# A two-layer hybrid step on one core: the engines' order from the scheduler's finer timing model, with three kinds of loads kept in program order

## The chip, the cores and the metric

The kernel runs on one core of one Trainium2 chip. The core has four compute engines, each with its own in-order queue of instructions: PE (TensorE, matmul), DVE (VectorE), ACT (ScalarE) and POOL (GpSimd). SP (SyncE) issues most of the loads. PE's weight loads are listed apart, as PEld. The metric is device time in microseconds (us) of one execution; lower is better. The time given is the median of several runs, and one further execution is recorded with a profile.

## What is computed

The reference is one inference step of a two-layer trunk on 640 tokens (512 latent, 128 context) of width 1024. Layer 0 mixes tokens with gated attention (16 query heads, 4 key/value heads of width 64), layer 1 with a gated linear recurrence in both directions (8 heads of width 128). Each layer modulates its input by a linear map of a conditioning vector and ends in a layer norm over the scaled residual.

```python
for i in range(DEPTH):
    sh_p, sc_p, g_p = _adaln(c_ctx, ada_w[i], ada_b[i])
    sh_s, sc_s, g_s = _adaln(c, ada_w[i], ada_b[i])
    hp = xp * (1.0 + sc_p) + sh_p
    hs = xs * (1.0 + sc_s) + sh_s
    if i % N_MIXERS == 0:
        out_p, kp, vp = _attn_context(hp, ...)
        out_s = _attn_latent(hs, cache_k, cache_v, ...)
    else:
        out_p, sp_fw, sp_bw = _rec_mix(hp, zeros, zeros, ...)
        out_s, _, _ = _rec_mix(hs, state_fw, state_bw, ...)
    xp = _layer_norm(DEEPNORM_ALPHA * xp + g_p * out_p, ...)
    xs = _layer_norm(DEEPNORM_ALPHA * xs + g_s * out_s, ...)

# _rec_mix, per head and direction, chunk by chunk
o_i = scores(q_i, k_i, decay) @ v_i + (q_i * exp(b_i)) @ S
S = exp(b_last) * S + (k_i * exp(b_last - b_i)).T @ v_i
```

It returns the tokens after both layers, the new keys and values of the context tokens, and the new recurrent states.

## The kernel before

**Number format.** Each fp32 operand of a large product is split into a high part, a cast, and a low part, the remainder. A product is then three matmuls: high by high, low by high, high by low. The function `split_piece` does this for weights: ACT casts a loaded piece `raw` of 128x1024 into the high part (L215), another engine subtracts to get the low part (L216).

**Loads.** Weights come in pieces of 512 KB in one fixed list, `order`, on SP's queue. `pump` issues the next loads of the list whenever fewer than two pieces are waiting (eight at the start). The list holds x and the modulation weights first (`"x"`, `"ada_w0"`, `"attn_kv"`), then the attention's input weights, the rest of the modulation weights (`"ada_w1"` among them), the attention's output weights, and last the recurrence's (`"rec_w_in"`, `"rec_w_out"`).

**Stages.** The lead-in (to about 150 us) transposes and modulates x, projects keys, values and the first queries (rows xps, adaps, acc, qps) and the gate path (gps). The attention (to 387 us) runs units of one head and 256 queries: scores sc, exponentials p, transposes pt, product with the values pot; the next queries (qmm, qps) and the modulation maps (adaps) run between them. Then the output projection, the layer norm and the transposed input of layer 1 follow (outp, h1t).

The recurrent layer (487.7 to 815.1 us in the profile) goes over 8 heads. `proj_gen` projects a head: 5 weight pieces, first two for value and gate (vgps, L1090 to L1092), then three for q and the two forget gates (rps, L1100 to L1102), 48 rps matmuls for each third. `evac` takes a third out of its bank: a sigmoid s on ACT (L1122), for the gates also a second sigmoid s2 (L1132), and products on DVE. The weight pieces use a ring of two buffers (rhi, rlo; one of the pieces goes to wspare), so a cast into rhi needs the matmuls that read the buffer's last content done.

`gla_gen` is a head's lane, which runs beside the next head's projection. It has 7 levels: at each, lv matmuls on PE (L1230, from the sixth level on L1236) read a copy kc of the keys that ACT makes (L1208) and the scaled queries; DVE scales the keys (kv, L1239), squares the decays (L1243), scales the queries (qv, L1244) for the next level, and merges the scores into near (L1220). After the fifth level comes dg (L1254). Then kp transposes the keys (L1270), ACT copies them to kt (L1272), sp takes kt times v (L1276), op forms the output (L1293 to L1296), on is normed and multiplied by the gate on DVE (L1307), and oT transposes it (L1312).

The last head's lane has no projection beside it. The tail (`tail_gen`) runs there: the splits of the output weights, gateps (L288) and 84 outp matmuls of layer 1 for the heads that are ready. Then the last outp matmuls, the layer norm and the stores follow.

**What sets the order.** The program is traced in the order in which the Python code calls its instructions, and a lane is woven into a projection by due times in us (`Lane`, `D_GLA` to `D_OUT`, `weave`). The framework's scheduler then decides the order of each engine's instructions, within what the data allow, by a timing model. `tc.keep_in_program_order(ins)` ties an instruction to the one traced before it on the same engine, so that the two are not exchanged. Some instructions are tied in this way already (L513, L675, L749, L1328 and others).

Of the kernel before, what the change touches and what calls it, by code (L numbers as in the profile page):

```python
# [18 lines left out]
P = 128  # L19
D = 1024  # L20
KT = D // P
TS = 4
# [109 lines left out]
def hybrid_step(ctx: ExitStack, tc: tile.TileContext, a: dict, o: dict):  # L132
    nc = tc.nc
# [54 lines left out]

    ahead = deque()
    order = deque()  # L190

    def pump():
        while order:
            start = order[0] in FIRST
            if len(ahead) >= (RAW_START if start else RAW_AHEAD):
                break
            src = order.popleft()
            if src[0] == "x":
                c = slice(src[1] * CW, (src[1] + 1) * CW)
                nc.sync.dma_start(xt[:, :TS, c], a["xs"][:, c].rearrange("(t p) d -> p t d", p=P))  # L200
                nc.sync.dma_start(xt[:, TS, c], a["xp"][:, c])
                continue
            raw = (raw0 if start else rawp).tile([P, 1024], F32, tag="raw", name="raw")
            nc.sync.dma_start(raw, piece(src))
            ahead.append((src, raw))

    def piece(src):
        name, c, i = src
        return a[name][c][:, i * 1024:(i + 1) * 1024]

    def split_piece(hi, lo, src, lo_eng=None):
        pump()
        got, raw = ahead.popleft()
        assert got == src, (got, src)
        nc.scalar.copy(hi, raw)  # L215
        (lo_eng or nc.gpsimd).tensor_tensor(lo, raw, hi.bitcast(F32), ALU.subtract)  # L216
        pump()
# [28 lines left out]
    def take(src):  # L246
        pump()
        got, raw = ahead.popleft()
        assert got == src, (got, src)
        return raw  # L250
# [118 lines left out]
    def lpool(name, bufs):  # L369
        return left.enter_context(pool(name, bufs))  # L370
# [8 lines left out]
    xt = gsp.tile([P, TT, D], F32, tag="gs", name="xt")  # L379
# [1010 lines left out]
    xp = lpool("xp", 3)  # L1390
# [102 lines left out]
```

## Time and profile before

| | us |
|---|---|
| median of 3 runs (lowest, highest) | 907.76 (903.08, 910.23) |
| the profiled execution, its own time | 908.88 |
| span of its trace | 907.1 |
| mean granted TensorE clock | 0.982 |
| PE's last instruction to the end of the span | 9.3 |

The span is what the trace covers; the 1.8 us between it and the execution's own time lie around it. The page counts busy time per engine: engines work side by side, so the shares do not add up to 100%. "Idle before" is the time an engine stood ahead of an instruction, with the engine that released it. The granted clock is the share of full speed at which TensorE was allowed to run.

### The profile page before, as it was taken

The numbers are of one execution on the slowest core, as the hardware profiler recorded it, in microseconds if no ns is written. First come the engines' busy times: TensorE is split into PE (matmuls) and PEld (weight loads), VectorE is DVE, ScalarE is ACT, GpSimd is POOL, SyncE is SP. The second block draws the span as 40 slices with busy tenths as digits, with TensorE's granted clock in tenths as the row PEclk, the third lists the DMA queues.
The fourth block names the chain that finished last, engine by engine and source line by source line (L and its number), as shares of the span: only waits on it lengthen the run. The fifth ranks groups of instructions, "written<-read, shape, count | busy, mean of one in ns | idle before, by whom it ended". The sixth has DMA issues, their size and how long they took to land.

```text
span 907.1 us, 19250 instructions
## 1 busy us (share of the span) xinstructions
PE 856.6 (94%) x8116; PEld 745.8 (82%) x8116; DVE 542.8 (60%) x966; ACT 374.1 (41%) x735; POOL 213.9 (24%) x251
## 2 busy tenths in 40 slices
PE   5999899989989989999999999999999999998995
PEld 3679899857867845677889999999999999996774
DVE  3466334654655644567634758585858575859485
ACT  1142346543555644632243444444444444344200
POOL 2014001421323443440000133324141404120110
PEclk9999899998999999999999999999999999998998
DMA  9832120024024036264122322323132332223121
GB/s 316 306 127 82 47 70 25 1 92 142 1 91 142 1 118 220 81 209 151 45 95 69 93 84 78 96 59 108 56 101 82 87 91 87 83 70 136 53 94 69
DMA packets 32678, 89.86 MB, mean 99 GB/s; under 512 B 4400, under 2 KB 11568, under 8 KB 32592
## 3 DMA queue, kind: packets, MB, share of 16 engines
q1 hardware_dynamic: 21984, 71.57, 23.3%
q0 software_dynamic: 3264, 9.51, 3.9%
q10 hardware_dynamic: 7344, 7.55, 2.7%
q8 instruction: 64, 1.05, 0.5%
q14 instruction: 22, 0.18, 0.1%
HBM read 79.44 MB, written 9.18 MB: 98 GB/s over the span
## 4 chain that ended last, share of the span: by engine, by line
PE 80%; DVE 7%; DMA 5%; ACT 3%; POOL 3%; issue 2%; SPq 0%; ACTq 0%; DVEq 0%; POOLq 0%
PE rps L1100 7%; PE rps L1101 6%; PE rps L1102 6%; PE vgps L1090 4%; PE pot L744 4%; PE vgps L1091 4%; PE vgps L1092 4%; DMA raw<-in_ada_w 4%; PE pt L826 4%; PE outp L978 3%; PE outp L979 3%; PE outp L980 3%; PE adaps L258 3%; PE lv L1230 2%; PE sc L717 2%; PE gps L315 2%
## 5 line engine op out<-in xcount | busy, mean ns | idle before, releaser
L1100 PE MATMUL rps<-h1hi,rhi 128*128 128x320 f32 x368 | 117.2, 319 | 0.0
L1101 PE MATMUL rps<-h1lo,rhi 128*128 128x320 f32 x368 | 113.6, 309 | 0.0
L1102 PE MATMUL rps<-h1hi,rlo 128*128 128x320 f32 x368 | 113.5, 309 | 0.0
L819 POOL TENSOR_SCALAR p<-p,rc 128x640 f32<-128x640 f32 x64 | 52.1, 816 | 112.2 <-DVE rc L818 109.3
L1100 PEld LDWEIGHTS rps<-h1hi,rhi 128*128 128x128 f32 x368 | 69.1, 188 | 1.3
L814 ACT ACTIVATE p<-sc,nm 128x640 f32<-128x640 f32 x64 | 51.1, 798 | 44.7 <-DVE nm L811 34.4
L1101 PEld LDWEIGHTS rps<-h1lo,rhi 128*128 128x128 f32 x368 | 69.1, 188 | 0.0
L1102 PEld LDWEIGHTS rps<-h1hi,rlo 128*128 128x128 f32 x368 | 69.1, 188 | 0.0
L811 DVE TENSOR_REDUCE nm<-sc 128x1 f32<-128x640 f32 x64 | 52.4, 820 | 24.2 <-PE sc L718 23.5
L216 DVE TENSOR_TENSOR rlo<-raw,rhi 128x1024 fp32r<-128x1024 f32 x32 | 46.1, 1441 | 34.2 <-ACT rhi L215 34.2
L1258 POOL COPY At<-near 32x160 f32<-32x160 f32 x32 | 14.0, 438 | 198.0 <-DVE near L1220 197.0
L1208 ACT COPY kc<-A 128x640 f32<-128x640 f32 x40 | 32.2, 804 | 59.3 <-DVE A L1239 51.4
L215 ACT CAST rhi<-raw 128x1024 fp32r<-128x1024 f32 x32 | 33.6, 1049 | 52.8 <-PE rps L1101 47.7
L826 PE MATMUL pt<-small,p 128*128 128x128 f32 x320 | 52.6, 285 | 1.5 <-DVE pts L722 0.8
L1090 PE MATMUL vgps<-rhi,h1hi 128*128 128x256 f32 x180 | 51.3, 285 | 1.2 <-ACT h1hi L932 1.2
L1092 PE MATMUL vgps<-rhi,h1lo 128*128 128x256 f32 x180 | 50.4, 280 | 0.4 <-DVE h1lo L933 0.4
L1091 PE MATMUL vgps<-rlo,h1hi 128*128 128x256 f32 x180 | 50.6, 281 | 0.0
L744 PE MATMUL pot<-pts,vv 128*64 128x256 f32 x320 | 50.0, 390 | 0.0
L722 ACT COPY pts<-pt 128x512 f32<-128x512 f32 x64 | 36.1, 587 | 32.1 <-PE pt L826 31.8
L826 PEld LDWEIGHTS pt<-small,p 128*128 128x128 f32 x320 | 37.8, 144 | 13.4 <-issue 7.1
L258 PE MATMUL adaps<-raw,sil 128*32 128x256 f32 x384 | 33.7, 429 | 11.2 <-DMA raw<-in_ada_w 10.6
L717 PE MATMUL sc<-kk,X 128*128 128x320 f32 x128 | 43.8, 350 | 0.4 <-ACT p L814 0.4
(261 smaller groups left out, 2436.9 us busy)
## 6 DMA issues: line engine op xcount, KB each, us to landing
raw<-in_ada_w SPq DMA_DIRECT2D x48, 512.0 KB, 5.0
raw<-in_rec_w_in SPq DMA_DIRECT2D x40, 512.0 KB, 3.5
raw<-in_attn_w_in SPq DMA_DIRECT2D x16, 512.0 KB, 4.0
raw<-in_attn_w_out SPq DMA_DIRECT2D x8, 512.0 KB, 3.6
raw<-in_rec_w_out SPq DMA_DIRECT2D x8, 512.0 KB, 3.3
x1d<-y SPq DMA_DIRECT2D x5, 512.0 KB, 3.1
rx<-x1d POOLq DMA_DIRECT2D x20, 128.0 KB, 3.7
x1a<-rx POOLq DMA_DIRECT2D x20, 128.0 KB, 2.6
```

The costliest lines, as they stand in the source:

```text
L258: nc.tensor.matmul(ps[32 * q:32 * q + 32, :CW], sil[:, 4 * i + q, :], raw[:, q * CW:(q + 1) * CW], start=(i == 0), stop=(i == 1))
L717: nc.tensor.matmul(out, X[:, h, t0:t0 + P], kk[:, c, k0:k1], start=True, stop=False)
L744: nc.tensor.matmul(pot[j * HD:(j + 1) * HD, :CW], vv[:, slot, c * HD:(c + 1) * HD], moving[j], start=first, stop=last)
L811: nc.vector.tensor_reduce(nm[:, 0:1], sc[:, :, :320], AX.XY, ALU.max, negate=True)
L819: nc.gpsimd.tensor_scalar(p, p, rs[:, 0:1], 1.0, ALU.mult, ALU.mult)
L826: nc.tensor.transpose(pt[:, i * 256 + q * P:i * 256 + (q + 1) * P], ps[q][:, (k0 + i) * P:(k0 + i + 1) * P], ident)
L1090: nc.tensor.matmul(out, h1hi[:, k, t], hi, start=(k == 0), stop=False)
L1091: nc.tensor.matmul(out, h1hi[:, k, t], lo, start=False, stop=False)
L1092: nc.tensor.matmul(out, h1lo[:, k, t], hi, start=False, stop=(k == KT - 1))
L1100: nc.tensor.matmul(ps[:, j, :320], hi[:, k, :], h1hi[:, k, t], start=(k == 0), stop=False)
L1101: nc.tensor.matmul(ps[:, j, :320], hi[:, k, :], h1lo[:, k, t], start=False, stop=False)
L1102: nc.tensor.matmul(ps[:, j, :320], lo[:, k, :], h1hi[:, k, t], start=False, stop=(k == KT - 1))
```

## The change

Three edits. In `hybrid_step`, `pin` is a short name for `tc.keep_in_program_order` and `pass_on` a function that does nothing. In `pump`, loads of x and of all pieces whose name does not begin with "rec" go through `pin`. In `kernel`, the scheduler is told to decide with its finer timing model. All line numbers from L191 on are one higher in the changed kernel.

```diff
     ahead = deque()
     order = deque()
+    pin, pass_on = tc.keep_in_program_order, lambda ins: ins
...
-                nc.sync.dma_start(xt[:, :TS, c], a["xs"][:, c].rearrange("(t p) d -> p t d", p=P))
-                nc.sync.dma_start(xt[:, TS, c], a["xp"][:, c])
+                pin(nc.sync.dma_start(xt[:, :TS, c], a["xs"][:, c].rearrange("(t p) d -> p t d", p=P)))
+                pin(nc.sync.dma_start(xt[:, TS, c], a["xp"][:, c]))
                 continue
             raw = (raw0 if start else rawp).tile([P, 1024], F32, tag="raw", name="raw")
-            nc.sync.dma_start(raw, piece(src))
+            (pass_on if src[0][:3] == "rec" else pin)(nc.sync.dma_start(raw, piece(src)))
...
-    with tile.TileContext(nc) as tc:
+    with tile.TileContext(nc, schedule_with_timeline_sim=True) as tc:
         hybrid_step(tc, a, o)
```

No instruction is added or removed. Of the rows that each engine runs, 4011 stand elsewhere on PE, 673 on DVE, 325 on ACT, 37 on POOL and none on SP. Three places follow, with the order before and then the order now.

Place 1 is ACT in one head of the recurrent layer, from the fifth level's kc (copy of the keys) to the sigmoids of the second third. Before:

```order
L1208 COPY kc<-A 128x640
L215 CAST wspare<-raw 128x1024
L215 CAST rhi<-raw 128x1024
L1263 COPY At<-lv 32x5x32 x4
L1122 ACTIVATE s<-rps 128x640
L1263 COPY At<-lv 64x5x64 x2
L1272 COPY kt<-kp 128x1024
L215 CAST rhi<-raw 128x1024
L1122 ACTIVATE s<-rps 128x640
L1132 ACTIVATE s_6174<-rps 128x640
L1133 ACTIVATE A<-s_6174,omlb 128x640
```

And now:

```order
L216 CAST wspare<-raw 128x1024
L216 CAST rhi<-raw 128x1024
L1123 ACTIVATE s<-rps 128x640
L1209 COPY kc<-A 128x640
L1264 COPY At<-lv 32x5x32 x4
L1264 COPY At<-lv 64x5x64 x2
L216 CAST rhi<-raw 128x1024
L1123 ACTIVATE s<-rps 128x640
L1133 ACTIVATE s_6174<-rps 128x640
L1273 COPY kt<-kp 128x1024
L1134 ACTIVATE A<-s_6174,omlb 128x640
```

The copy kc moved behind the two casts and the sigmoid, and the copy kt behind the next cast and two sigmoids.

Place 2 is PE in the same head, around dg, where the fifth level (L1230, now L1231) ends and the sixth (L1236, now L1237) begins. Before, with 18 rps rows behind dg, of which three are shown:

```order
L1102 MATMUL rps<-h1hi,rlo 128x320
L1230 MATMUL lv<-A,kc 32x32 x20
L1254 MATMUL dg<-q,kd 32x32 x20
L1100 MATMUL rps<-h1hi,rhi 128x320
L1101 MATMUL rps<-h1lo,rhi 128x320
L1102 MATMUL rps<-h1hi,rlo 128x320
```

And now:

```order
L1103 MATMUL rps<-h1hi,rlo 128x320
L1231 MATMUL lv<-A,kc 32x32 x20
L1255 MATMUL dg<-q,kd 32x32 x20
L1237 MATMUL lv<-A 32x32 x20
L1101 MATMUL rps<-h1hi,rhi 128x320
L1102 MATMUL rps<-h1lo,rhi 128x320
```

The 18 rps rows between dg and the sixth level are gone from there; the rps row ahead of the fifth level's lv, the 30th of the 48 of its third before, is now the last of them. Further on in the same head, kp and sp, between which 12 rps rows stood, follow each other now:

```order
L1103 MATMUL rps<-h1hi,rlo 128x320
L1271 MATMUL kp<-small,A 128x128 x8
L1277 MATMUL sp<-v,kt 128x128 x8
L1101 MATMUL rps<-h1hi,rhi 128x320
L1102 MATMUL rps<-h1lo,rhi 128x320
```

Here, too, the rps row ahead of kp is the last of its third.

Place 3 is PE in the last head's lane, from the fourth level's lv on. Before, with outp rows (L978 to L980) between all steps:

```order
L1230 MATMUL lv<-A,kc 32x32 x20
L288 MATMUL gateps<-small,gcol_77 128x128 x4
L980 MATMUL outp<-whi,glo 128x512
L978 MATMUL outp<-w_9572,ghi 128x512
L979 MATMUL outp<-w_9572,ghi 128x512
L980 MATMUL outp<-w_9572,glo 128x512
L978 MATMUL outp<-whi,ghi 128x512
L979 MATMUL outp<-wlo,ghi 128x512
L980 MATMUL outp<-whi,glo 128x512
L978 MATMUL outp<-w_9572,ghi 128x512
L1230 MATMUL lv<-A,kc 32x32 x20
L1254 MATMUL dg<-q,kd 32x32 x20
```

And now:

```order
L981 MATMUL outp<-w_9573,glo 128x512
L1231 MATMUL lv<-A,kc 32x32 x20
L289 MATMUL gateps<-small,gcol_77 128x128 x4
L1231 MATMUL lv<-A,kc 32x32 x20
L1255 MATMUL dg<-q,kd 32x32 x20
L1237 MATMUL lv<-A 32x32 x20
L1237 MATMUL lv<-A 64x64 x10
L289 MATMUL gateps<-small,gcol_77 128x128 x4
L1271 MATMUL kp<-small,A 128x128 x8
L1277 MATMUL sp<-v,kt 128x128 x8
```

All 84 outp rows that run beside the lane now stand ahead of the fourth level's lv; before, 38 of them did.

## The prediction

> **What bounds the kernel now.** I read the page's head and its chain first, to see which engine sets the end.
>
> ```profile
> span 907.1 us, 19250 instructions
> PE 856.6 (94%) x8116; PEld 745.8 (82%) x8116; DVE 542.8 (60%) x966; ACT 374.1 (41%) x735; POOL 213.9 (24%) x251
> PE 80%; DVE 7%; DMA 5%; ACT 3%; POOL 3%; issue 2%; SPq 0%; ACTq 0%; DVEq 0%; POOLq 0%
> ```
>
> PE is busy for 94% of the span and is 80% of the chain that ended last. The program can become faster only where PE waits or where its clock is reduced, and it becomes slower wherever a new order makes PE wait. So I went to the table of busy time by stretch (columns: stretch, length, PE, PEld, DVE, ACT and POOL busy with counts, granted clock, DMA share, GB/s): six stages, then six short windows around PE's waits.
>
> ```profile
> 0.00:57.50 57.50, 45.20 (x291) 31.49 (x291) 23.76 (x50) 13.65 (x18) 7.66 (x15) 1.00 0.79 270
> 57.50:150.00 92.50, 88.20 (x617) 86.23 (x617) 42.60 (x72) 36.59 (x68) 10.64 (x6) 0.96 0.19 65
> 150.00:387.00 237.00, 223.28 (x1710) 167.61 (x1708) 130.94 (x294) 123.18 (x269) 81.54 (x84) 0.97 0.26 88
> 487.70:815.10 327.40, 327.06 (x4330) 316.01 (x4328) 219.54 (x341) 148.44 (x294) 90.36 (x124) 1.00 0.28 83
> 815.10:859.80 44.70, 38.39 (x478) 31.37 (x478) 31.48 (x51) 17.42 (x35) 4.74 (x8) 0.92 0.29 98
> 859.80:907.10 47.30, 36.67 (x156) 28.60 (x155) 34.46 (x61) 0.80 (x1) 5.95 (x7) 0.95 0.21 78
> ...
> 89.56:92.97 3.41, 1.53 (x11) 1.19 (x11) 2.69 (x5) 0.95 (x2) 0.00 (x0) 1.00 0.00 0
> 92.97:99.80 6.83, 4.45 (x17) 4.46 (x18) 1.56 (x4) 2.96 (x5) 0.00 (x0) 0.50 0.00 1
> 816.60:820.00 3.40, 0.74 (x5) 0.50 (x5) 3.37 (x5) 3.28 (x6) 0.00 (x0) 1.00 0.95 352
> 820.00:826.84 6.84, 6.05 (x83) 4.85 (x87) 6.08 (x8) 4.68 (x6) 0.00 (x0) 0.50 0.69 249
> 322.00:325.40 3.40, 1.70 (x18) 0.98 (x18) 1.74 (x5) 1.29 (x3) 3.40 (x4) 1.00 0.00 0
> ...
> 534.10:580.88 46.78, 46.78 (x621) 45.23 (x621) 32.71 (x50) 21.30 (x43) 15.64 (x21) 1.00 0.27 83
> ```
>
> Two things are to be seen. The recurrent layer (487.7 to 815.1) has no PE idle time at all: 327.06 of 327.40 us. One head of seven takes 46.78 us there (last row), all of it PE. And a wait can cost twice: where PE was busy for only 1.53 of 3.41 us, or 0.74 of 3.40, the next 6.83 us ran at a granted clock of 0.50; where it was busy for 1.70 of 3.40 us, the clock stayed at 1.00.
>
> **The change, part by part.** The pins are the cheap part. SP's rows stand in the same order before and after, so no load is moved past another on its queue; I cost them at nothing, from both sides, since the DMA share is 0.28 where PE is full. What counts is the second part: 4011 PE, 673 DVE, 325 ACT and 37 POOL rows stand elsewhere. Almost all moves are harmless swaps of matmuls; what costs is where PE's next row now needs something that is not ready. I followed each moved row to its producer.
>
> *The recurrent layer, places 1 and 2 of the change.* Today nothing there waits on PE, and ACT is the engine that waits for PE:
>
> ```profile
> PE lv L1236 <- DVE A L1244: 0.3, 1, 0.3
> ...
> ACT rhi L215 <- PE rps L1101: 42.8, 20, 4.2
> ...
> ACT kt L1272 <- PE kp L1270: 26.1, 7, 3.7
> ```
>
> The second row (us in total, times, longest) is the key: ACT's cast of the next weight piece stands until PE has run the last rps matmul that reads the buffer. ACT has queued idly there for 42.8 us and hurt nobody, because kc, kt and what else the lane needs stood ahead of it. In the new order they stand behind it, and behind the sigmoid of the whole rps. These rows of one head, from the timeline (start, us, engine, line, idle before), give the durations:
>
> ```profile
> 554.11 0.73 ACT L1208 COPY kc<-A 128x640 f32<-128x640 f32 x1 [2.72 <-DVE A L1239]
> 559.53 1.05 ACT L215 CAST rhi<-raw 128x1024 fp32r<-128x1024 f32 x1 [3.50 <-PE rps L1101]
> 560.48 1.17 ACT L1263 COPY At<-lv 32x160 f32<-32x160 f32 x4
> 561.67 0.70 ACT L1122 ACTIVATE s<-rps 128x640 f32<-128x640 f32 x1
> 567.50 1.01 ACT L1272 COPY kt<-kp 128x1024 f32<-128x1024 f32 x1 [3.74 <-PE kp L1270]
> 554.87 0.83 DVE L1244 TENSOR_TENSOR A<-A,Tb 128x640 f32<-128x640 f32 x1 [0.60 <-ACT kc L1208]
> 555.73 0.82 DVE L1239 TENSOR_TENSOR A<-A,T 128x640 f32<-128x640 f32 x1
> 556.47 0.20 DVE L1243 TENSOR_TENSOR Tb<-T 128x40 f32<-128x40 f32 x1
> 558.45 0.34 DVE L1220 COPY_PREDICATED near<-masks,lv 128x160 f32<-128x160 uint8 x1
> 555.88 0.53 PE L1230 MATMUL lv<-A,kc 128*32 128x32 f32 x38
> 566.43 1.04 PE L1270 MATMUL kp<-small,A 128*128 128x128 f32 x8
> ```
>
> Wait 1, ahead of the fifth level's lv. PE runs all 48 rps rows of a third; then come in series the cast (559.53 to the next start 560.48: 0.95), the sigmoid 0.70, kc 0.73 and DVE's qv 0.82 to 0.83, and only then lv can start. All rps rows in front are done, so nothing covers it: 0.95 + 0.70 + 0.73 + 0.82 = 3.2 us of PE idle. DVE's weight split, now ahead of qv, runs beside the sigmoid and kc. Wait 2, between dg and the sixth level: the same rows now stand back to back without 18 rps rows between, while DVE needs kv 0.82 (0.74 to the next start), T 0.20, near 0.34 and qv 0.82, some 2.15 us, against 0.95 of lv and dg: 1.2 us idle. Wait 3, between kp and sp: kt now stands behind cast, sigmoid and the second sigmoid (another 0.70), so 1.05 + 0.70 + 0.70 + 1.01 with small overlaps, 3.25 us after the third's end, less the kp pitch of 0.8: 2.4 us, where twelve rps rows covered kt before. Elsewhere in the head at least 20 rps or vgps rows still cover each step. Sum: 3.2 + 1.2 + 2.4 = 6.8 us per head, 47.6 us for the seven heads, whose new rows are alike.
>
> Next the clock. Waits 1 and 2 stand within 5.4 us with 0.95 us of work between: any 3.4 us laid into them at the worst place has PE busy for about 1.0, below the 1.53 of the window at 89.56, so I expect 6.83 us at 0.50 behind them. In such a stretch a gps matmul took 0.47 us where it takes 0.31 (rows below), and some of the stretch falls into idle time: I take 2.2 us lost. Wait 3 alone is nearer to the lone waits that changed nothing (1.70 of 3.40 busy) but larger: 0.8 us on average. 3.0 us a head, 21 us in all. Bounds for a head: only a third of the waits real and no clock loss, 2 us; all of it with both throttles full, 13 us; I take 9.8, since the terms come from rows of the same head.
>
> [...]
>
> *The last head's lane and the tail (place 3).* Before, the 84 outp rows were spread among the lane's levels; now all 84 run ahead of the fourth level, and nothing but gateps stands in the chain behind it.
>
> ```profile
> 816.61 0.74 PE L1312 MATMUL oT<-small,on 128*128 128x128 f32 x5 [1.49 <-DVE on L1307]
> 820.79 0.76 PE L1230 MATMUL lv<-A,kc 128*32 128x32 f32 x40 [3.45 <-ACT kc L1208]
> 835.05 0.56 PE L1230 MATMUL lv<-A,kc 128*32 128x32 f32 x40
> 854.98 0.40 PE L979 MATMUL outp<-w,ghi 128*128 128x512 f32 x1
> 855.22 0.39 PE L980 MATMUL outp<-w,glo 128*128 128x512 f32 x1
> 859.04 0.74 PE L1312 MATMUL oT<-small,on 128*128 128x128 f32 x5 [1.33 <-DVE on L1307]
> ```
>
> From the fourth level (835.05) to oT (859.04) the lane takes 24.0 us, set by ACT and DVE steps, with 46 outp rows of 0.23 us (854.98 to 855.22) beside it. Moved ahead, they push 835.05 back by 46 × 0.23 = 10.6 us, and the five weight splits (1.22 us each) that DVE now runs ahead of the lane's steps add about 1. The lane itself takes no less. With long gaps between its few PE rows I expect half clock there: some 4 us on its 12 us of PE work and 2.5 on the outp rows behind oT, less about 1 for the wait behind oT that shrinks. Together +17 (bounds 11, the shift alone, and 22).
>
> *Gains ahead of it.* In the lead-in PE's wait of 1.81 us at 91.32 gets 24 gps rows to cover it:
>
> ```profile
> 91.32 1.11 PE L572 MATMUL qps<-identr,qs 128*128 128x128 f32 x8 [1.81 <-DVE qs L565]
> 95.35 0.63 PE L315 MATMUL gps<-hhi,whi 128*128 128x320 f32 x1 [2.41 <-ACT X L574]
> 95.78 0.47 PE L316 MATMUL gps<-hlo,whi 128*128 128x320 f32 x1
> 89.20 0.31 PE L317 MATMUL gps<-hhi,wlo 128*128 128x320 f32 x1
> ```
>
> That frees up to 4.2 us of idle and 2 of half clock; I take 4. In 150 to 387 us PE is idle for 13.7 us (237.00 less 223.28); scores are issued earlier between the adaps rows, of which I take 3 us. In the first 57.5 us a group of transposes fills part of a wait: 1. Together −8; bounds −2 (new waits eat it) and −14.
>
> **Sum.** 47.6 + 21 + 17 − 8 = +77.6 on the profiled execution's 908.88: 986.5 us. The median of the runs shown is 907.76, a tenth of a per cent lower, so I predict 986.
>
> **The rivals.**
> A: the waits come, the clock does not fall. 47.6 + 10.5 in the tail (17 less 6.5) − 8 = +50: 959 us. [...] For it: in most of the kernel lone waits left the clock at 1.00. Against: the windows at 89.56 and 816.60.
> B, the other side: kc and kt are ready when PE arrives, so that heads still take 46.8 us. This decides if the 3.2 us behind the third's last rps row shrink to under the pitch of one rps row, that is if cast and sigmoid do not hold ACT. Then the early gain of 8 and a tail of at most a few us remain: 901 to 908. Against it: ACT's order is fixed, and the waits table shows the cast waiting 20 times for just that row.
> C: the order changes but PE's full stages absorb it, 908: the seven heads would have to keep their 94% at no idle; the same rows speak against it.
> D: both throttles fall fully in each head (13 × 7 = 91) and the tail takes 22: 908.88 + 91 + 22 − 8 = 1014.
>
> **How the numbers follow.** My forecast (about 970 to 1005 by itself) gets 0.62, A with waits partly covered (930 to 970) 0.22, D 0.08, B 0.04, C 0.04. The range 945 to 1010 leaves out B, C, the lower third of A and half of D, about 2 in 10. A measurement of this kernel can tell about 1% from no change: faster by more than that only by the good half of B, 0.02; within 1%, 0.05; slower 0.93.
>
> **What would show it.** In the changed profile: each recurrent head takes about 56.6 us from rps end to rps end, with PE waits named lv <- DVE A (L1245) of about 3.2 and 1.2 us and sp <- ACT kt (L1273) of about 2.4 us, seven of each; granted clock 0.50 for a window or two in each head, so a mean near 0.93 in that stage; from the fourth lv of the last head to oT 24 to 28 us without outp rows; the 1.81 us wait ahead of qps gone. If heads stay at 46.8 us, B or C holds; if they take 53 to 54 at clock 1.00, A does. I would be wrong in sign if ACT's cast no longer waited for PE's rps.

## The result and the profile after

| | us |
|---|---|
| after, median of 4 runs (lowest, highest) | 979.13 (977.34, 979.46) |
| before, runs beside them on the same chips included, median of 4 | 906.82 (903.08, 910.23) |
| ratio of the two, 95% interval | 1.0794 (1.0748 to 1.0840) |
| the profiled execution after, and its span | 977.34, 975.6 |

The changed kernel is 7.9% slower. The head of its page, with PE's granted clock by slices and the chain:

```profile
span 975.6 us, 19232 instructions
PE 877.9 (90%) x8116; PEld 767.2 (79%) x8116; DVE 538.0 (55%) x966; ACT 372.8 (38%) x735; POOL 209.2 (21%) x251
PEclk9999999999999999999989889898989979889898
PE 79%; DVE 8%; ACT 5%; DMA 4%; issue 1%; POOL 1%; SPq 0%; ACTq 0%; DVEq 0%; POOLq 0%
```

Every engine runs the same rows as before; the 18 instructions that the page counts fewer are semaphore instructions. PE does its work in 21 us more of busy time, at a reduced clock in the second half (0.93 in the heads, where it was 1.00), and is also idle for longer. The stages tell where. The table of busy time by stretch, before, cut at the same instructions in both kernels: last pmm to last gps (lead-in), to the first outp (attention), then first vgps with the whole input to oT of the seventh head (heads), to oT of the last head, to the end:

```profile
78.96:148.05 69.09, 64.79 (x451) 64.14 (x450) 26.69 (x43) 26.38 (x50) 5.33 (x2) 0.95 0.16 55
148.05:387.22 239.17, 225.23 (x1725) 169.56 (x1724) 132.44 (x295) 125.31 (x272) 81.75 (x85) 0.97 0.26 87
...
462.42:816.61 354.19, 351.90 (x4497) 340.14 (x4497) 231.81 (x356) 161.79 (x313) 91.64 (x126) 1.00 0.28 85
816.61:859.04 42.43, 37.60 (x472) 30.58 (x472) 30.00 (x49) 15.91 (x34) 3.46 (x5) 0.92 0.29 99
859.04:907.10 48.06, 37.43 (x161) 29.36 (x161) 34.46 (x61) 0.80 (x1) 5.95 (x7) 0.95 0.21 77
```

The same stages after:

```profile
77.61:140.37 62.76, 62.38 (x451) 62.19 (x450) 28.98 (x48) 26.65 (x51) 5.43 (x3) 1.00 0.19 62
140.37:372.44 232.07, 221.88 (x1725) 165.91 (x1724) 131.43 (x295) 125.72 (x271) 84.67 (x85) 0.99 0.28 89
...
447.45:871.86 424.41, 376.65 (x4497) 363.51 (x4497) 227.27 (x357) 161.34 (x315) 85.12 (x126) 0.93 0.25 71
871.86:924.54 52.68, 39.01 (x471) 32.85 (x472) 29.03 (x48) 14.39 (x31) 3.52 (x5) 0.87 0.21 74
924.54:975.60 51.06, 38.78 (x161) 30.77 (x161) 34.33 (x61) 0.79 (x1) 5.72 (x7) 0.90 0.20 73
```

Heads +70.2, the last lane +10.2, the end +3.0, lead-in −6.3, attention −7.1, and about −1.5 elsewhere: together +68.5, the difference of the spans. PE's waits in the heads, by the table of waits (us in total, times, longest), are new:

```profile
PE lv L1231 <- DVE A L1245: 22.1, 7, 3.2
PE sp L1277 <- ACT kt L1273: 16.4, 7, 2.3
PE lv L1237 <- DVE A L1245: 5.5, 7, 1.0
```

Seven of each, 44.0 us. One head in the timeline (start, us, engine, line, idle before) shows how each comes about:

```profile
552.99 1.05 ACT L216 CAST rhi<-raw 128x1024 fp32r<-128x1024 f32 x1 [1.83 <-PE rps L1102]
553.95 0.70 ACT L1123 ACTIVATE s<-rps 128x640 f32<-128x640 f32 x1
554.54 0.71 ACT L1209 COPY kc<-A 128x640 f32<-128x640 f32 x1
568.84 1.04 ACT L216 CAST rhi<-raw 128x1024 fp32r<-128x1024 f32 x1 [2.69 <-PE rps L1102]
569.91 0.70 ACT L1123 ACTIVATE s<-rps 128x640 f32<-128x640 f32 x1
570.51 0.70 ACT L1133 ACTIVATE s<-rps 128x640 f32<-128x640 f32 x1
571.09 1.02 ACT L1273 COPY kt<-kp 128x1024 f32<-128x1024 f32 x1
554.07 1.23 DVE L217 TENSOR_TENSOR rlo<-raw,rhi 128x1024 fp32r<-128x1024 f32 x1 [0.67 <-ACT rhi L216]
555.29 0.82 DVE L1245 TENSOR_TENSOR A<-A,Tb 128x640 f32<-128x640 f32 x1
556.26 0.76 PE L1231 MATMUL lv<-A,kc 128*32 128x32 f32 x40 [3.15 <-DVE A L1245]
558.28 0.76 PE L1237 MATMUL lv<-A 128*32 128x32 f32 x40 [0.73 <-DVE A L1245]
572.16 2.10 PE L1277 MATMUL sp<-v,kt 128*128 128x128 f32 x12 [2.35 <-ACT kt L1273]
```

PE ends the third; ACT casts, runs the sigmoid, copies kc; DVE scales the queries; only then lv runs, after 3.15 us. kt ends at 572.11, behind the cast and two sigmoids, and sp waits 2.35 us for it. At 554.07 DVE's weight split stands ahead of the scaling: it ends when kc does, at 555.3. That detail matters below.

### The profile page after: what moved, and what is told of

It is laid out like the page before. It is cut to its first block, busy times and chain, and to the rows that moved or that the text cites. A ratio compares the mean times of both kernels' runs of the same rounds, so it can differ in the third digit from the quotient of the medians.

```text
span 975.6 us, 19232 instructions
## 1 busy us (share of the span) xinstructions
PE 877.9 (90%) x8116; PEld 767.2 (79%) x8116; DVE 538.0 (55%) x966; ACT 372.8 (38%) x735; POOL 209.2 (21%) x251
## 4 chain that ended last, share of the span: by engine, by line
PE 79%; DVE 8%; ACT 5%; DMA 4%; issue 1%; POOL 1%; SPq 0%; ACTq 0%; DVEq 0%; POOLq 0%
PE rps L1101 7%; PE rps L1102 7%; PE rps L1103 6%; PE pot L745 4%; PE vgps L1091 4%; PE vgps L1092 4%; PE vgps L1093 4%; PE pt L827 3%; DMA raw<-in_ada_w 3%; PE adaps L259 2%; PE outp L979 2%; PE outp L980 2%; PE outp L981 2%; PE sc L718 2%; PE sp L1277 2%; PE gps L316 2%
## 5 line engine op out<-in xcount | busy, mean ns | idle before, releaser
L1101 PE MATMUL rps<-h1hi,rhi 128*128 128x320 f32 x368 | 124.8, 339 | 0.2 <-issue 0.2
L1102 PE MATMUL rps<-h1lo,rhi 128*128 128x320 f32 x368 | 122.4, 333 | 0.0
L1103 PE MATMUL rps<-h1hi,rlo 128*128 128x320 f32 x368 | 120.2, 327 | 0.0
L1101 PEld LDWEIGHTS rps<-h1hi,rhi 128*128 128x128 f32 x368 | 76.5, 208 | 1.8 <-issue 0.6
L1102 PEld LDWEIGHTS rps<-h1lo,rhi 128*128 128x128 f32 x368 | 76.1, 207 | 0.3
L1103 PEld LDWEIGHTS rps<-h1hi,rlo 128*128 128x128 f32 x368 | 75.9, 206 | 0.0
L1259 POOL COPY At<-near 32x160 f32<-32x160 f32 x32 | 18.4, 576 | 237.8 <-DVE near L1221 236.8
L217 DVE TENSOR_TENSOR rlo<-raw,rhi 128x1024 fp32r<-128x1024 f32 x32 | 42.0, 1313 | 31.0 <-ACT rhi L216 31.0
L1209 ACT COPY kc<-A 128x640 f32<-128x640 f32 x40 | 32.1, 802 | 54.5 <-DVE A L1240 34.0
L1240 DVE TENSOR_TENSOR A<-A,T 128x640 f32<-128x640 f32 x32 | 26.4, 825 | 43.1 <-PE lv L1237 32.8
L1231 PE MATMUL lv<-A,kc 128*32 128x32 f32 x1600 | 23.7, 206 | 26.3 <-DVE A L1245 23.6
```

What stands on the lines that cost most here:

```text
L1101: nc.tensor.matmul(ps[:, j, :320], hi[:, k, :], h1hi[:, k, t], start=(k == 0), stop=False)
L1102: nc.tensor.matmul(ps[:, j, :320], hi[:, k, :], h1lo[:, k, t], start=False, stop=False)
L1103: nc.tensor.matmul(ps[:, j, :320], lo[:, k, :], h1hi[:, k, t], start=False, stop=(k == KT - 1))
```

## The experiments

The theory: PE waits where its next row's input stands behind other rows on ACT and DVE with nothing to run meanwhile, and half clock follows from that idle time. The rivals: PE's order alone does it; ACT's and DVE's queues alone do it; half clock comes on its own. Where an order of before or after is imposed, a list of row numbers per engine (left out here) feeds this function, called behind `hybrid_step`; each engine is named with the part of the program. The lists and wrappers added in this way shift the line numbers, so that each fence has those of its own kernel:

```diff
+def in_order(tc, engine, runs):
+    ins = [i for i in tc.nc.cur_bb.bb.instructions if i.engine == engine]
+    row = [ins[n] for s, k in runs for n in range(s, s + k)]
+    info = mybir.DependencyInfo(mybir.DependencyClass.NoSync, mybir.DependencyReason.DATA)
+    for a, b in zip(row, row[1:]):
+        tc.add_manual_dep(b, a.name, info, reason="in_order")
```

Ratios are to the kernel before on the same chip, with 95% intervals. The changed kernel was not run again beside the experiments, so a time set against its 979.13 us compares chips; the median of the kernel before lay between 901.87 and 906.82 us on them.

**The pins alone.**

```diff
-    with tile.TileContext(nc, schedule_with_timeline_sim=True) as tc:
+    with tile.TileContext(nc) as tc:
```

> The loads kept in program order, without the finer timing model. PE's and SP's orders are then those of before, ACT's differs in 5 rows and DVE's in 4. Theory (the finer model's order is the whole effect): the time of before, 907 us, within 5 us. Rival (the pinned loads cost or gain something by themselves): more than 5 us away from 907.

Measured: 902.22 us beside 905.19, ratio 0.9967 (0.9941 to 0.9994). The loss is in the timing model's order, not in the pins; the interval just leaves out no change, so the pins may gain a few tenths of a per cent by themselves.

**The finer model without the pins.** This edit is to the kernel before.

```diff
-    with tile.TileContext(nc) as tc:
+    with tile.TileContext(nc, schedule_with_timeline_sim=True) as tc:
```

> The finer timing model without the three pins on the loads. SP's order then changes in 19 rows, all of them in the first loads: pieces of attn_w_in and a chunk of x are queued ahead of attn_kv and ada_w pieces that the start needs. The other engines stand as in the changed kernel but for a few rows (PE 219, DVE 86, ACT 15). Theory (the pins keep the finer model from moving loads, and matter only there): the start grows by one to three pieces of 512 KB at the 316 GB/s of the first slice, 1.7 us each, so 2 to 6 us: 979 to 986, with the heads at 56 us as in the changed kernel. Rival (loads wait in SP's queue anyway, the pins change nothing): 975 to 979 and the same start.

Measured: 987.9 us, ratio 1.0934 (1.0881 to 1.0988). Its size is a little beyond what was expected and its place is not as expected at all: the start is the same (last pmm at 78.57 us, 77.61 in the changed kernel). The first row of the output projection is 4.3 us late, 3.4 of it from the attention (235.46 us for 232.07, at a granted clock of 0.97 for 0.99). The larger part of the loss, 8.3 us up to the first row of the heads, lies in the output projection, which waits:

```profile
395.13 0.80 PE L978 MATMUL outp<-wohi,hhi 128*128 128x512 f32 x1 [6.00 <-DVE y L998]
```

DVE's y stands there behind weight splits, for which ACT had waited 8.7 us for loads of attn_w_out. Why the scheduler orders that stage otherwise when early loads are free was not settled. So the pins did save some 9 us within the changed kernel, at a place far behind the first loads, the only ones whose order they change.

**One sigmoid behind kc and kt.** PE's rows in the heads stay as they are.

```diff
-            nc.scalar.activation(halves(s[:]), pv, AF.Sigmoid)
+            pin(nc.scalar.activation(halves(s[:]), pv, AF.Sigmoid))
```

> The changed kernel with one pin more: the first sigmoid of each third keeps its place in program order on ACT. PE's order in the heads stays as in the changed kernel; on ACT kc and kt now stand ahead of the sigmoids, still behind the cast of the weights. Theory (each ACT row ahead of kc or kt adds its duration to PE's wait): the 3.15 us wait at lv falls by one sigmoid, 0.70, to about 2.45; the 2.34 us wait at sp by two, to about 0.95; the wait behind dg stays at 0.4 to 1.0. That is 2.1 us a head, 15 in all, and up to 10 more if the clock falls less: 953 to 965 us. Rival (PE's order alone makes the waits, ACT only follows it): waits and time unchanged, 975 to 982.

Measured: 966.57 us, ratio 1.0671 (1.0615 to 1.0727). The waits in the heads:

```profile
PE lv L1231 <- DVE A L1245: 21.5, 7, 3.1
PE sp L1277 <- ACT kt L1273: 8.1, 7, 1.2
```

The wait at sp fell by half, as each row ahead of kt counts. The wait at lv hardly fell, though kc now ran before the sigmoid. The timeline of one head shows why:

```profile
549.82 1.04 ACT L216 CAST rhi<-raw 128x1024 fp32r<-128x1024 f32 x1 [2.55 <-PE rps L1102]
550.77 0.72 ACT L1209 COPY kc<-A 128x640 f32<-128x640 f32 x1
550.89 1.22 DVE L217 TENSOR_TENSOR rlo<-raw,rhi 128x1024 fp32r<-128x1024 f32 x1 [0.78 <-ACT rhi L216]
552.03 0.82 DVE L1245 TENSOR_TENSOR A<-A,Tb 128x640 f32<-128x640 f32 x1
```

kc ended at 551.49, but DVE was in the weight split until 552.1. The split was as long as sigmoid and kc together; with one path shortened the other sets the wait, and so the time came out a little above the 953 to 965 us of the theory.

**ACT and DVE in the order of before in the seven heads, PE as in the changed kernel** (`in_order` on PE, ACT and DVE).

> The changed kernel with PE's order as it is, but ACT's and DVE's orders in the seven heads as in the kernel before. Theory (ACT's and DVE's queues ahead of kc, qv and kt make a part of the waits, PE's row without cover the rest): the wait at the fifth level's lv falls from 3.15 to about 2.1 us (from lv to lv the lane takes 3.29 us in the kernel before, less lv and 5 rps rows), the one behind dg stays at about 1, the one at sp falls from 2.34 to about 1.15: 4.2 us a head for 6.3, and 1 to 3 us of half clock: a head of 52 to 54 us, 945 to 960. Rival 1 (PE's order makes all of it): no gain, above 972. Rival 2 (ACT's and DVE's orders make all of it): a head near 46.8, 905 to 915.

Measured: 957.65 us, ratio 1.0588 (1.0552 to 1.0623). The waits:

```profile
PE lv L1288 <- DVE A L1296: 12.2, 7, 1.9
PE lv L1282 <- DVE A L1296: 12.1, 7, 2.1
PE sp L1328 <- ACT kt L1324: 7.8, 7, 1.2
```

L1282 is the fifth level's lv, L1288 the sixth's. 32.1 us remain of 44.0. So the two queues make a quarter of the waits; the rest stays under PE's own order (lv, dg, lv and kp, sp back to back), which leaves these rows without cover. Neither rival holds by itself. The sum was near the expected one, 4.6 us a head for 4.2, the split among the first two waits was not: 1.7 and 1.7 where 2.1 and about 1 were expected. The other half, PE in the order of before with ACT and DVE as in the changed kernel, was not run; the next experiment comes nearest to it.

**PE kept in program order from the heads on, ACT, DVE and POOL left to the finer model.** The engine is wrapped so that `pin` is put around each of its calls; the next experiment does the same with ACT.

```diff
+    nc = KeptCore(nc, pin, ('tensor',))
     residual = Residual()
```

> The changed kernel, but PE keeps program order from the recurrent layer's heads on (tail included); the other engines stay with the finer model. Theory (the 70 us in the recurrent layer and the 13 in the tail are PE rows put where their inputs are not ready, the 15 us gained ahead of it are independent of that): a head takes 46.8 us again at clock 1.00, the tail 90 us, and 975.6 - 70 - 13 = 892 us of span, 894 in time, below both kernels. Rival A (ACT's queue makes the waits, whatever PE's order): the waits at lv and sp stay, some 2 us or more a head, 910 or above. Rival B (the gain ahead was borrowed, loads or buffers only moved forward): heads back at 46.8, but 905 or above.

Measured: 916.92 us, ratio 1.0112 (1.0067 to 1.0157): 62 us come back, but 23 fewer than expected. The waits in the heads (L139 is the line of the wrapper):

```profile
PE lv L139 <- DVE A L1266: 8.2, 12, 1.1
```

The two stretches behind oT of the seventh head:

```profile
813.27:859.33 46.06, 34.77 (x460) 28.38 (x460) 29.80 (x49) 15.49 (x33) 2.45 (x5) 0.91 0.26 93
859.33:916.38 57.05, 43.25 (x173) 33.55 (x173) 35.18 (x61) 0.79 (x1) 5.34 (x7) 0.89 0.19 65
```

The heads take 364 us, 10 more than before: program order is not the order of before, it has 12 rps rows where that has 18 ahead of the fifth level. And the tail is 103 us, as in the changed kernel: in program order 12 outp rows fewer cover the lane. Whether DVE's order adds to that was not tried. The mistake was to take program order for the old order; the gain ahead was kept, as the first outp at 373.76 us shows.

**ACT kept in program order from the heads on.**

> The changed kernel, but ACT keeps program order from the recurrent layer's heads on; the scheduler then also places PE's rows otherwise (38 rps rows, lv, 10 rps, lv, dg, lv, 2 rps, lv of 10; 12 rps between kp and sp). Theory: sp waits no longer (12 rps rows of 0.147 us cover kt's 1.0), the wait ahead of the fifth level falls to about 0.6 to 1.0 us, the one behind dg stays near 1.0, and a new one of about 1 us stands ahead of the seventh level, where 2 rps rows replace 24. Some 3 us a head, so 21 us in place of 70 and a tail between the two: 920 to 940 us. Rival (PE's place for lv, not ACT's queue, makes the waits): waits of 6 us a head remain and the time stays above 960.

Measured: 1082.1 us, ratio 1.1944 (1.1891 to 1.1997). Far from both theories. The waits in the heads:

```profile
PE rps L1122 <- ACT rhi L139: 52.0, 10, 6.3
PE vgps L1112 <- ACT rhi L139: 22.3, 7, 3.2
```

The lane no longer waits for ACT much; the projection does. In program order the cast of the next weights stands behind the lane's copies and the sigmoid, and PE runs out of weights. The scheduler placed PE's rows anew in this run, so it does not separate the two engines. What it shows with the changed kernel is that ACT carries two streams here, and that PE waited for whichever stood behind the other.

**Matmuls in the waits.** The changed kernel's order on every engine, with rows whose result is overwritten or unread: 20, 4 and 15 a head.

```diff
+        def fill(ps, n):
+            for _ in range(n if h < RH - 1 else 0):
+                nc.tensor.matmul(ps[:, :320], h1hi[:, 0, :P], h1hi[:, 0, :320], start=True, stop=True)
...
             pt = wide(bank2("lv"))
+            fill(pt, {4: 20, 5: 4}.get(lev, 0))
...
         sp = bank2("sp")
+        fill(wide(sp), 15)
```

> The changed kernel with its own order on every engine in the heads and the tail, and matmuls whose result nobody reads put into PE's three waits of each of the seven heads: 20 ahead of the fifth level's lv, 4 ahead of the sixth's, 15 ahead of sp, of 0.147 us each, so 2.9, 0.6 and 2.2 us of PE work in waits of 3.15, 0.4 to 1.0 and 2.34 us. Theory (of the 9.6 us that a head is longer, 6.3 are the waits and 3.3 are half clock that follows from PE's idle time): the waits do not change, the granted clock stays at 1.00 in the heads, a head takes 53.1 to 53.5 us, the time falls by 20 to 23 us to 956 to 960. Rival (the half clock comes at its own times, or PE's pitch is lower there for another cause): no gain, 977 to 985.

Measured: 957.83 us, ratio 1.0599 (1.0558 to 1.0640): more work, 21 us less time. One head in the table by stretch, in the changed kernel and then here:

```profile
502.02:558.28 56.26, 50.04 (x619) 48.35 (x620) 31.64 (x50) 21.00 (x42) 12.09 (x17) 0.92 0.26 72
502.00:555.35 53.35, 52.82 (x659) 50.92 (x659) 31.67 (x50) 21.00 (x42) 12.10 (x17) 1.00 0.27 75
```

What is left of the waits in seven heads (L1302 is the sixth level's lv):

```profile
PE lv L1302 <- DVE A L1310: 1.1, 5, 0.2
PE sp L1343 <- ACT kt L1338: 1.1, 7, 0.2
```

A head took 56.4 us in the changed kernel (from 500.09 to 838.62 us, six heads) and 53.35 here, at a granted clock of 1.00. So 3.1 us a head were half clock, and PE's idle time caused it.

**The tail in the order of before** (`in_order` on all four engines for what is traced in the tail).

> The changed kernel, but what is traced in the tail (the output weights' splits, gateps, outp, the last norms; the last lane's own steps as far as they are traced there) stands in the order of the kernel before on every engine; the seven heads as in the changed kernel. Theory (the outp rows ahead of the fourth level and the weight splits ahead of the lane make the tail's 13.2 us): from the last projected head's oT to the end 90 to 92 us for 103.7, time 964 to 967. Rival (the tail's loss is in the steps behind oT, at half clock and in waits for DVE's y, as it was where PE alone kept program order): 972 to 979.

Measured: 965.53 us, ratio 1.0683 (1.0639 to 1.0727). The last lane and the end:

```profile
876.03:917.00 40.97, 37.33 (x471) 30.54 (x472) 28.68 (x48) 14.21 (x31) 3.46 (x5) 0.92 0.26 96
917.00:965.00 48.00, 37.42 (x161) 29.39 (x161) 34.46 (x61) 0.80 (x1) 5.66 (x7) 0.94 0.22 77
```

89.0 us for 103.7: the tail's whole loss is the order there.

**Lead-in, and attention, in the order of before** (`in_order` on all four engines, one stage each).

> The changed kernel, but what is traced in the lead-in (first queries, gps, keys) stands in the order of the kernel before on every engine. Theory (6.3 of the 15 us gained ahead of the heads come from the lead-in, where 24 gps rows cover the wait at qps): from the last pmm to the last gps 69.1 us again for 62.8, with waits of 1.8 and 2.4 us and half clock behind them, 985 us. Rival (the gain lies in the attention alone): no change, 977 to 980.

Measured: 988.02 us, ratio 1.0945 (1.0893 to 1.0996), 8.9 more than the changed kernel; the lead-in takes 70.9 us for 62.8, with waits of 3.56 us at qps and 2.40 behind it. It took 69.1 us in the kernel before, where the first of these waits was 1.81.

> The changed kernel, but what is traced between the lead-in and the heads' first projection (scores to transposes of the input of layer 1) stands in the order of the kernel before on every engine. Theory (7.1 us of the gain come from the attention, where fewer and shorter waits for ada_w and qps lie among PE's rows): from the last gps to the first outp 239 us for 232.1, 986 us. Rival (the attention gains only because the lead-in ended sooner and its loads were ahead): 977 to 980.

Measured: 981.13 us, ratio 1.0862 (1.0799 to 1.0925), 2.0 more, and the two ratios' intervals overlap; the attention takes 233.2 us for 232.1, not 239. The pins-alone kernel, whose PE rows stand as before, has 233.1 there too. What the profile of before had there and these two had not is this:

```profile
202.20:212.44 10.24, 9.42 (x50) 6.37 (x51) 1.34 (x5) 2.68 (x5) 1.84 (x2) 0.50 0.42 148
```

10.24 us at a granted clock of 0.50, some 5 us lost by an estimate from these two numbers, in one profile of the four with that order. The other three took 233.1 to 233.8 us in the stage. The nine profiles with the finer order and the pins took 230.2 to 234.0, so that no worth of the attention's order is shown beyond about 1 us.

**Before's order from the heads on, and the finer order in the lead-in alone** (`in_order` on all four engines).

> The changed kernel up to the recurrent heads, from there to the end every engine in the order of the kernel before. Theory (the loss lies all in the order of that part, the gain ahead of it does not depend on it): heads of 46.8 us, last oT to end 48 us, span 975.6 - 70.2 - 13.2 = 892, time 894 (890 to 898), faster than both. Rival (what was gained ahead comes back as later waits there): 903 or above.

Measured: 895.55 us, ratio 0.9905 (0.9872 to 0.9939), faster than both kernels. Heads, last lane and end:

```profile
449.74:803.98 354.24, 351.73 (x4497) 340.06 (x4497) 231.84 (x356) 161.90 (x313) 91.64 (x126) 1.00 0.29 84
803.98:845.51 41.53, 36.70 (x471) 30.09 (x472) 29.81 (x49) 15.85 (x33) 3.46 (x5) 0.92 0.29 101
845.51:893.50 47.99, 37.40 (x161) 29.40 (x161) 34.45 (x61) 0.80 (x1) 5.65 (x7) 0.93 0.22 79
```

> The finer model's order up to the end of the lead-in, the order of the kernel before on every engine from there to the end. Theory (the lead-in alone makes the gain that repeats, 8 to 9 us; the attention's part of the difference between the two profiles was mostly a clock reduction of 10 us in the profiled execution of before, its order is worth 1 to 2): as fast as the kernel with the finer order in the attention too, 0.990 to 0.993 of before, 895 to 899 us, and from the last gps to the first outp 233 to 235 us. Rival (the attention's order is worth the 7 us that the two profiles differ by there): 0.996 or above, 901 us or more, 239 us in that stage.

Measured: 897.17 us, ratio 0.9937 (0.9912 to 0.9963), with 233.8 us in the attention. The time and the stage are as the theory had them, the ratio a little above its 0.993. The two intervals overlap, and the lead-in takes 62.7 to 62.8 us in every profile with its finer order: it carries most of the gain that repeats. Both kernels have the pins as well, which alone had a ratio of 0.9967; a part of the gain may be theirs.

## Why the prediction was right

Predicted 986 us, measured 979.13. Between the two profiles the terms are off by +1.6 us in the heads, −3.8 in the tail and −7.0 ahead of them, so the time is not close because errors cancel. Point by point:

- *Bound.* Right: PE had no idle time in the heads, and only the order could take or give any.
- *Waits in the heads.* Predicted 3.2, 1.2 and 2.4 us, measured 3.15, 0.79 and 2.34 on average: 6.3 a head for 6.8, each at its predicted instruction and releaser. The second was 0.98 to 1.02 us in the four heads whose lv and dg ran at full clock, and 0.40 to 0.73 in the three where half clock had already set in, so that lv and dg covered more of DVE's steps. The sigmoid path was named as the limit. That is half of it: DVE's split path, said to run beside it, is as long, which the sigmoid experiment showed.
- *Clock.* 3.0 us a head predicted, 3.1 shown by the filled waits: 6.83 us at half clock behind the wait at lv in each of the seven heads, and 3.41 behind the wait at sp in four. Rival A, waits without half clock, is out, and so is D, which had half clock cost 6.2 us a head. The expectation for the lead-in put half clock behind both of its waits. In the kernel before, by the rows shown with the prediction, the gap of 1.81 us stood alone ahead of the half clock at 92.97 us; the one of 2.41 us ended at 95.35 us, within it. So one gap was enough there, and the wait at sp, 2.34 to 2.35 us, was enough in four of seven heads, as the last section shows.
- *Heads in all.* 68.6 predicted, 70.2 measured. That measure includes a growth of 1.6 in the wait ahead of the seventh head's oT (3.08 us for 1.49), which the prediction had no term for.
- *Tail.* 17 predicted, 13.2 measured, of which 10.2 in the lane. The shift of the fourth level's lv, some 10.6 net, came as 9.5: from the seventh head's oT to that lv the lane takes 27.9 us for 18.4. The 2.5 behind the last oT came as 3.0. The term that was too large is the 4 us for half clock between that lv and oT: the clock did fall there, from 1.00 to 0.86, but the stretch grew only from 24.0 to 24.8 us, with PE busy for 13.8 of them, as PE's slower rows fell into idle time. That the order is the cause is shown by the tail of before: 89.0 us for 103.7.
- *Gains ahead.* −8 predicted, −15.0 between the two profiles. The lead-in was undersized, 4 for the 6.3 to 8.1 that its stage shows. The attention's 3 was oversized for the order itself, of which no more than about 1 is shown; most of the 7.1 that the profiles differ by is a clock reduction that the profiled execution of before happened to have. Without it the early gain is about 10.
- *The pins at nothing.* Right to within some tenths of a per cent against the kernel before, with its order; not in company with the finer model, where leaving them out costs 9 us by another order of later stages.
- *Rivals B and C.* Heads that still take 46.8 us were made by putting all engines back to the order of before, and the time was then 895.55. Nothing of it happened in the changed kernel, whose heads took 56.4.

## What to carry to other kernels

When a scheduler reorders engines, follow for each PE row the rows now queued ahead of its producers on ACT and DVE; a row there that itself waits for PE's last matmul turns a covered chain into a serial one (3.15 us of wait ahead of lv here), and shortening one of two equal paths gained almost nothing here (3.07 us were left on average). Count a PE wait with the half clock that it can bring, here half as much again (3.1 us on 6.3). An order that gains in one stage and loses in another can be had for the first alone: the finer order up to the heads and the old one from there took 1% less time than the kernel before and 8.5% less than the changed one.

## What the runs showed of the hardware

In the profile before and in the one after, all changes of the granted clock lie a whole number of steps of 3.41 us apart. In the steps below the fall to half clock went with PE's busy time within one step, not with the length of a gap. Three pairs of steps of the changed kernel, around the wait at sp in the first and second head and the wait at lv in the first (length and PE busy first, the granted clock third from the end):

```profile
511.67:515.08 3.41, 2.63 (x21) 2.38 (x19) 0.69 (x1) 1.74 (x3) 0.00 (x0) 1.00 0.00 0
515.08:518.50 3.42, 1.86 (x17) 1.86 (x17) 1.89 (x3) 2.23 (x4) 0.00 (x0) 1.00 0.48 145
569.70:573.11 3.41, 1.06 (x10) 0.95 (x9) 2.57 (x3) 3.11 (x5) 0.00 (x0) 1.00 0.25 35
573.11:576.53 3.42, 3.42 (x17) 3.42 (x17) 1.38 (x6) 0.00 (x0) 0.00 (x0) 0.50 0.29 119
498.02:501.43 3.41, 0.91 (x80) 0.83 (x80) 3.38 (x6) 1.06 (x2) 0.00 (x0) 1.00 0.42 130
501.43:508.26 6.83, 6.24 (x61) 6.21 (x62) 3.39 (x7) 1.13 (x4) 4.44 (x8) 0.50 0.35 67
```

The first head's wait of 2.34 us fell across two steps, with PE busy for 2.63 and 1.86 us of them, and the clock stayed. The second head's, of 2.35 us, fell into one step, 1.06 us busy, and the next step ran at half clock. So the same wait costs more in one head than in the next: heads took 55.9 to 56.2 and 56.8 to 57.1 us in turn. The two profiles hold 502 steps at full clock, from the first record of the clock (24.70 us before, 23.57 us after) on: all 17 with at most 1.50 us of PE work were followed by half clock, none of the 475 above 2.05 us, and 4 of the 10 between. Of these ten busy time does not tell which: the step at 89.56 us before, with 1.53 us, was followed by half clock, those at 627.73 and 740.37 us after, with 1.53 and 1.52 us, were not.
